# Far values: another order of seven block products, other buffers for two of x's sums, and near scores at later steps, in a hybrid attention and state-space layer

## Chip, cores and metric

The kernel runs on one core of a Trainium2 chip. The metric is the device time of one execution in microseconds (us); a kernel's time is the median of its runs. Engines are named as the profile names them: PE is TensorE (its weight loads are PEld), DVE is VectorE, ACT is ScalarE, POOL is GpSimd, SP is SyncE.

## What is computed

One decoder layer in float32 on 512 tokens of width 1024, cut here to what the change touches:

```python
proj = x @ w_in[layer]                       # q, k, v for 3 groups, ssm input, gate logits
q = apply_rope(q, pos); k = apply_rope(k, pos)
for g, (window, dilation) in enumerate(((128, 1), (512, 4), (2048, 16))):
    o_g, lse_g = dilated_group_attention(q[:, :, g], k[:, :, g], v[:, :, g], window, dilation)
attn = merge_by_softmax_denominators(outs, lses)
y_s = s5_ssm(u, ...)                         # complex diagonal scan, then GELU and GLU
mixed = gates[0] * (attn @ w_attn_br) + gates[1] * (y_s @ w_ssm_br)
h = layer_norm(ALPHA * x + mixed @ w_out)
out = layer_norm(ALPHA * h + swiglu(h))
```

Group 0 of the attention is called near, groups 1 and 2 are called far.

## The kernel before

**Precision and weights.** Each float32 operand of a matmul is split into a rounded part (hi) and a remainder (lo), and a product is three matmuls: hi by hi, hi by lo, lo by hi (line 207). A weight block of 128x1024 is prepared by a cast on ACT (names `whi…` and `wx…`) and a subtraction on DVE (`wlo…`, or the second half of `wx…`). SP loads the raw weights ahead. Prepared blocks lie in three pairs of buffers and, for the far values, in two borrowed ones, of which one is used once. When PE has used a block, `w.release()` gives its buffer to the next block in the list, so a block is prepared four units ahead of its use.

**Order of the work.** Every engine works through its own instructions in the order in which the code records them. The code goes through numbered steps: 4 to 28 are input projections, 28 to 36 the far values (7 products of 2 units each, 8/14 step a unit), 36 to 56 the other projections as five "quads" of 7 products (4/7 step a product), and after that come GLU, branch and output projections and the feed-forward part. `at_step(n, fn)` enters other work into this order: `fn` is recorded ahead of the first unit or product whose step is n or more.

**Far values.** The product of x with the value weights of groups 1 and 2 is made by blocks with seven products instead of eight (`v_product`, line 1205), numbered 1 to 7 and taken in the order of `VORDER` (line 1163). A product is 24 matmuls of 128x512, 12 for each unit. Products 1, 2 and 3 take blocks of x as they are. The others take sums of blocks: product 5 takes sum 0, product 7 sum 1, product 6 sum 2 and product 4 sum 3. A sum (`sum_x`, line 1081) is made by ACT, which negates a block (line 1085), and by an accumulating transfer from POOL's queue (line 1086). Sum 2 needs sum 0, and sum 3 needs sum 2. `split_x` (line 1088) then makes hi by a cast on ACT and lo by a subtraction on DVE. The results are `x_hi`, `x_lo` (sum 0, in the place of a block of x that is no longer needed), `x23h` and `x23l` (sums 1 and 2) and `x4` (sum 3, hi and lo in one buffer). The products add up in three pairs of PSUM banks, `vx`, `vy` and `vz`; `v_evict` (line 1217) copies or adds a bank into the values `v` after products.

The value weights are four raw blocks `rv0` to `rv3`, loaded at line 1169; `rv2` becomes `rv2 + rv3` by `sum_v` (line 1191) on DVE, and `prepare_v` (line 1174) makes the seven operands from these one by one, with three more sums in place. Products 1 and 6 use `rv0`, product 2 uses `rv1`, product 5 uses the summed `rv2`.

**The state output.** The state-space branch leaves its output `ysb` in the buffer `gat0`. Sixteen transfers on SP's queue write it to DRAM (`turn_y`, line 754, names `ydr<-ysb`), and it is fetched again much later. SP's next work behind them are the loads of the first quad's weights (line 1125, `rq`).

**Buffers.** Large buffers are named `big0` to `big8` and `gat0` to `gat3`; code asks for them by `home(n)`, and a table `swapped` renames some of them from step 24.9 on (`swap_homes`, line 246). Before, it exchanges 2 with 5, gat0 with 7 and 6 with 8. So `x23h` (home 5) lies in big2, `x23l` (home 7) in gat0, where `ysb` was, and `x4` (home 8) in big6, where one half of the states was. PE reads the states last in step 23.

**Near attention.** For each pair of heads j there are scores on PE (`attn_scores`, at `SCORES[0][j]`), then a masked maximum on DVE (line 848) and an exponential on ACT (line 850) for eight pieces, transposes on PE (`attn_turn`, at `WEIGHTS[0][j]`) and the product with the values at the step of the next scores. In the profile these are `s`, `un`, `t` and `o`.

Of the kernel before, what the change touches and what calls it, by code (L numbers as in the profile page):

```python
# [45 lines left out]
NSTR = 16  # L46


SCORES = [[33.8, 36.3, 39.1, 41.9, 44.7], [49.9, 52.5, 54, 55.7, 58.2]]
WEIGHTS = [[35.2, 38.1, 40.9, 43.7], [51, 53.2, 55, 57.2]]  # L50

# [120 lines left out]
def emit(ctx, tc, i, out):  # L174
# [65 lines left out]
    def home(n, name, dt=F32):  # L240
        n = swapped.get(n, n)
        return gat(n[1:], name, dt) if isinstance(n, str) else big(n, name, dt)

    swapped = {}

    def swap_homes():
        for a, b in ((2, 5), ("g0", 7), (6, 8)):
            swapped[a], swapped[b] = b, a

    w = Weights(nc, wp, split)  # L250
    out_homes = deque(("g0", 2, 6, 3))
# [727 lines left out]
    def at_step(n, fn, *a):  # L979
        fill.setdefault(n, []).append((fn, a))  # L980
# [41 lines left out]
    for kind in range(2):  # L1022
        for j, n in enumerate(SCORES[kind]):
            if j > 0:
                at_step(n, attn_values, kind, j - 1)
            if j < NPAIR:
                at_step(n, attn_scores, kind, j)
                at_step(WEIGHTS[kind][j], attn_turn, kind, j)
    xn = []
# [80 lines left out]
    at_step(24.4, sum_x, 0)  # L1110
    at_step(24.4, sum_x, 1)
    at_step(24.9, swap_homes)
    at_step(25.9, sum_x, 2)
    at_step(27.4, sum_x, 3)
    for n, at_ in enumerate((28.1, 27.2, 28.6, 29.6)):
        at_step(at_, split_x, n)


# [41 lines left out]

        w.after = rest

    VORDER = (1, 2, 5, 6, 3, 7, 4)
    vraw, vops, vslot, vbank = {}, {}, {}, {}
    vleft = deque((n, u) for n in VORDER for u in range(2))

# [166 lines left out]
    for g in (1, 2):  # L1333
        vs[g] = home((3, "g1", 0)[g], f"v{g}").rearrange("p (b c) -> p b c", b=4)
    for n, m in enumerate(VORDER):
        for u in range(2):
# [31 lines left out]
    for n in range(4):  # L1368
        ws = w.views[N_GLU + n]
        bs = []  # L1370
        for e in range(2):
            b = glu(f"gl{n}{e}")
# [323 lines left out]
    for e, m, nxt in (("b", 5, 6), ("a", 7, 4)):  # L1696
        at_ = dn_prep.index((m, 2))
# [321 lines left out]
def build(inputs):  # L2019
    import concourse.bacc as bacc  # L2020

    a = {k: np.asarray(v) for k, v in inputs.items()}
    arrays = {f"in_{k}": np.ascontiguousarray(v) for k, v in {**layout(a), **constants()}.items()}
    nc = bacc.Bacc("TRN2", target_bir_lowering=False, num_devices=1)
    aps = {k[3:]: nc.dram_tensor(k, v.shape, mybir.dt.from_np(v.dtype), kind="ExternalInput").ap()
           for k, v in arrays.items()}
    out = nc.dram_tensor("out_dram", (S, D), F32, kind="ExternalOutput").ap()
    with tile.TileContext(nc) as tc:
        with ExitStack() as ctx:
            with tc.manual_schedule():  # L2030
                emit(ctx, tc, aps, out)
    return nc, arrays
# [8 lines left out]
```

## Time and profile before

| what | us |
|---|---|
| median of three runs (827.59, 830.01, 830.37) | 830.01 |
| the profiled execution, its own time | 832.69 |
| its span, first to last instruction | 830.9 |
| PE busy within the span | 807.5 |
| DVE busy | 667.8 |
| ACT busy | 412.5 |

Between the span and the execution's own time lie 1.8 us. A row of a timeline gives start, duration, engine, line, operation, `out<-in` with the program's names (buffer numbers left out), shapes and a count; a bracket gives how long the engine had been idle and what ended that. Durations of neighbouring rows overlap a little, since instructions are pipelined; the distance between two starts is what an instruction adds to its engine's time. The chain's rows give start, duration, engine, name, line and count.

### The profile page before, as it was taken

What the parts mean: (1) busy time and instruction counts of PE and PEld (TensorE: products, weight loads), DVE (VectorE), ACT (ScalarE), POOL (GpSimd) and SP (SyncE); (2) the same over time, 40 slices, a digit from 0 to 9 for tenths busy, and PEclk for the clock granted to TensorE, in tenths of its full rate; (3) what the DMA queues carried; (4) which work ended last, traced back from release to release, by engine and by line L of the source; (5) the groups of instructions that cost most, each with busy time, mean ns of one, the idle gap of its engine ahead of it and who ended that gap; (6) DMA issues with size and microseconds to landing.
All of it is one profiled execution on the core that took longest, in us unless ns stands there. A gap on an engine that the chain in (4) does not pass through costs nothing.

```text
span 830.9 us, 13774 instructions
## 1 busy us (share of the span) xinstructions
PE 807.5 (97%) x5584; PEld 724.5 (87%) x5584; DVE 667.8 (80%) x1059; ACT 412.5 (50%) x607; POOL 80.2 (10%) x98
## 2 busy tenths in 40 slices
PE   9999999995999999999999999999999999999995
PEld 7888888874799999988888899999999999888884
DVE  6977997958768979746886699887777789789986
ACT  5973332543475645775334155554555445554520
POOL 0000002240003212300000230000000000020104
PEclk9999999996999999999999999999999999999998
DMA  8743438791225455762524225332223333774553
GB/s 335 188 112 123 144 121 250 184 202 25 101 96 104 105 133 128 173 234 95 209 103 166 86 78 177 114 141 102 103 103 106 109 116 114 276 173 147 148 130 102
DMA packets 32047, 117.48 MB, mean 141 GB/s; under 512 B 7664, under 2 KB 12528, under 8 KB 22512
## 3 DMA queue, kind: packets, MB, share of 16 engines
q1 hardware_dynamic: 23808, 91.83, 31.9%
q0 software_dynamic: 6544, 23.07, 13.4%
q10 hardware_dynamic: 1632, 1.70, 0.6%
q8 instruction: 44, 0.72, 0.3%
q14 instruction: 19, 0.16, 0.1%
HBM read 100.60 MB, written 9.70 MB: 133 GB/s over the span
## 4 chain that ended last, share of the span: by engine, by line
PE 89%; DVE 3%; DMA 3%; ACT 2%; SPq 1%; POOL 1%; issue 1%; DVEq 0%; ACTq 0%
PE qx L1258 7%; PE dnx L1798 5%; PE dnz L1798 4%; PE qz L1258 3%; PE pu L614 3%; PE pg L208 3%; PE pg L210 3%; PE pg L209 3%; PE dny L1798 2%; DMA ydr<-ysb 2%; PE wo L210 2%; PE wo L208 2%; PE b L208 2%; PE b L210 2%; PE b L209 2%; PE wo L209 2%
## 5 line engine op out<-in xcount | busy, mean ns | idle before, releaser
L1598 ACT CAST whi<-sums 128x1024 fp32r<-128x1024 f32 x40 | 41.9, 1048 | 66.2 <-DVE sums L349 66.2
L202 DVE TENSOR_TENSOR wlo<-raw,whi 128x1024 fp32r<-128x1024 f32 x44 | 54.2, 1235 | 17.7 <-ACT whi L201 17.7
L201 ACT CAST whi<-raw 128x1024 fp32r<-128x1024 f32 x44 | 45.9, 1048 | 22.9 <-PE pk L209 17.4
L349 DVE TENSOR_TENSOR wlo<-sums,whi 128x1024 fp32r<-128x1024 f32 x40 | 48.7, 1219 | 0.0
L349 DVE TENSOR_TENSOR wlo_q<-rq,whi_q 128x1024 fp32r<-128x1024 f32 x28 | 34.2, 1222 | 17.7 <-ACT whi_q L1153 17.6
L1153 ACT CAST whi_q<-rq 128x1024 fp32r<-128x1024 f32 x28 | 29.3, 1051 | 37.6 <-DVE rq L349 29.3
L1798 PE MATMUL dnx<-whi_d,pc 128*128 128x512 f32 (+1 forms) x128 | 38.2, 376 | 0.0
L775 POOL DMA_DIRECT2D kq<-qz x32 | 25.3, 1604 | 129.1 <-DVE qz L349 94.1
L208 PE MATMUL pg<-x_hi,whi 128*128 128x512 f32 x96 | 37.6, 392 | 0.0
L209 PE MATMUL pg<-x_lo,whi 128*128 128x512 f32 x96 | 37.4, 390 | 0.0
L210 PE MATMUL pg<-x_hi,wlo 128*128 128x512 f32 x96 | 37.4, 389 | 0.0
L850 ACT ACTIVATE un<-un,st 128x256 f32<-128x256 f32 (+1 forms) x64 | 30.8, 484 | 12.8 <-DVE st L848 12.8
L965 ACT ACTIVATE gt<-pg,bgate 128x512 f32<-128x512 f32 x12 | 8.3, 690 | 41.8 <-PE pg L210 41.8
L1710 ACT CAST whi_d<-dn 128x1024 fp32r<-128x1024 f32 x16 | 16.9, 1054 | 23.0 <-DVE dn L349 11.0
L1798 PEld LDWEIGHTS dnx<-whi_d,pc 128*128 128x128 f32 x128 | 23.6, 188 | 4.4
L1720 POOL DMA_DIRECT2D whi_db<-in_w_dp x3 | 1.7, 577 | 246.1 <-PE dny L1798 242.4
L349 DVE TENSOR_TENSOR wlo<-ra,whi 128x1024 fp32r<-128x1024 f32 x20 | 24.4, 1220 | 0.4 <-ACT whi L1598 0.4
L1798 PE MATMUL dnx<-wlo_d,pc 128*128 128x512 f32 (+1 forms) x64 | 24.1, 376 | 0.0
L1258 PE MATMUL qx<-x23h,whi_q 128*128 128x256 f32 x80 | 23.2, 290 | 0.0
L1258 PE MATMUL qz<-x_hi,whi_q 128*128 128x256 f32 x80 | 22.8, 286 | 0.0
L1258 PE MATMUL qz<-x_hi,wlo_q 128*128 128x256 f32 x80 | 22.6, 283 | 0.0
L1258 PE MATMUL qz<-x_lo,whi_q 128*128 128x256 f32 x80 | 22.6, 283 | 0.0
(838 smaller groups left out, 2985.4 us busy)
## 6 DMA issues: line engine op xcount, KB each, us to landing
raw<-in_w_in SPq DMA_DIRECT2D x12, 1024.0 KB, 5.3
ra<-in_w_gu SPq DMA_DIRECT2D x10, 1024.0 KB, 4.7
rb<-in_w_gu SPq DMA_DIRECT2D x10, 1024.0 KB, 4.8
rq<-in_w_quad SPq DMA_DIRECT2D x16, 512.0 KB, 4.0
dn<-in_w_dq SPq DMA_DIRECT2D x8, 1024.0 KB, 4.8
rv<-in_w_in SPq DMA_DIRECT2D x4, 1024.0 KB, 8.7
kq<-qz POOLq DMA_DIRECT2D x32, 128.0 KB, 5.0
raw<-in_w_br SPq DMA_DIRECT2D x4, 1024.0 KB, 4.9
```

What stands on the lines that cost most here:

```text
L201: act.copy(hi, src)
L202: dve.tensor_tensor(lo, src, hi.bitcast(F32), op=ALU.subtract)
L208: pe.matmul(dst, a[0], b[0], start=first, stop=False)
L209: pe.matmul(dst, a[0], b[1], start=False, stop=False)
L210: pe.matmul(dst, a[1], b[0], start=False, stop=last)
L349: eng.tensor_tensor(o, a, b, op=op)
L775: pool.dma_start(dst[32 * q : 32 * q + 32], z[32 * (q ^ 1) : 32 * (q ^ 1) + 32], accum_op=ALU.add)
L850: act.activation(pt, pt, AF.Exp, bias=mneg, scale=-1.0, accum_out=zsum)
L1153: act.copy(hi, src)
L1258: pe.matmul(d[:, 256 * e : 256 * e + 256], p_[:, e, k, :], q_[:, k, :], start=(first and e == k == m == 0), stop=(k == 3 and m == 2), skip ...
L1598: act.copy(hi, src)
L1798: pe.matmul(acc[key][0 if key == "v" else e][:, cs], p_, q_[:, cs], start=(key, e) not in begun, stop=(m == 2), skip_group_check=True)
```

## The change

Four tables or numbers change, and no operation is added or removed.

```diff
-SCORES = [[33.8, 36.3, 39.1, 41.9, 44.7], [49.9, 52.5, 54, 55.7, 58.2]]
-WEIGHTS = [[35.2, 38.1, 40.9, 43.7], [51, 53.2, 55, 57.2]]
+SCORES = [[34.8, 38.2, 40.5, 42.8, 45.1], [49.9, 52.5, 54, 55.7, 58.2]]
+WEIGHTS = [[37.1, 39.4, 41.7, 44], [51, 53.2, 55, 57.2]]
...
     def swap_homes():
-        for a, b in ((2, 5), ("g0", 7), (6, 8)):
-            swapped[a], swapped[b] = b, a
+        swapped.update({2: 5, 5: 2, "g0": 7, 7: 6, 6: 8, 8: "g0"})
...
-    at_step(25.9, sum_x, 2)
-    at_step(27.4, sum_x, 3)
-    for n, at_ in enumerate((28.1, 27.2, 28.6, 29.6)):
+    at_step(26.4, sum_x, 2)
+    at_step(28.9, sum_x, 3)
+    for n, at_ in enumerate((28, 28.5, 30.2, 32)):
         at_step(at_, split_x, n)
...
-    VORDER = (1, 2, 5, 6, 3, 7, 4)
+    VORDER = (1, 5, 2, 6, 3, 7, 4)
```

Products 2 and 5 change places. `x23l` now lies in big6 and `x4` in gat0; `x23h` stays in big2. The negations for sums 2 and 3 and the four splits are recorded at other steps. The first near scores stand ahead of product 4 instead of between the two units of product 7; each of the four transposes stands two quad products behind its scores (the first: two units and two products), where three products (the first: two units) lay between them before.

On DVE, at the place where the far values begin, the rows before were these (`v20` is product 2, unit 0, and so on; `kq`, `zq` are the rotary products of the last two projections, `pq10` and `pq11`).

```order
L349 TENSOR_TENSOR wlo0_v20_1718<-rv1_1658,whi0_v20_1717 128x1024
L349 TENSOR_TENSOR kq01_1484<-pq11_1756,rope_130 128x4x128
L349 TENSOR_TENSOR zq10_1749<-pq11_1756,rope_130 128x4x128
L349 TENSOR_TENSOR wlo1_v21_1753<-rv1_1658,whi1_v21_1752 128x1024
L349 TENSOR_TENSOR rv0_1491<-rv2_1332,rv0_1491 128x1024
L349 TENSOR_TENSOR wlo2_v50_1788<-rv2_1332,whi2_v50_1787 128x1024
L349 TENSOR_TENSOR x23l_1793<-xf1_1582,x23h_1792 128x1024
L349 TENSOR_TENSOR rv0_1491<-rv2_1332,rv0_1491 128x1024
L349 TENSOR_TENSOR wx_v51_1816<-rv2_1332,wx_v51_1816 128x1024
L349 TENSOR_TENSOR x_lo0_95<-xf0_1580,x_hi0_93 128x4x256
```

After, in the same place (the changed file is one line shorter, so line 349 is 348 there), with the rows from the last subtraction of product 1 on:

```order
L348 TENSOR_TENSOR wx_v11_1666<-rv0_1491,wx_v11_1666 128x1024
L348 TENSOR_TENSOR rv0_1491<-rv2_1332,rv0_1491 128x1024
L348 TENSOR_TENSOR rv2_1332<-rv2_1332,rv3_1526 128x1024
L348 TENSOR_TENSOR kq01_1484<-pq10_1722,rope_130 128x4x128
L348 TENSOR_TENSOR zq10_1748<-pq10_1722,rope_130 128x4x128
L348 TENSOR_TENSOR wlo0_v50_1718<-rv2_1332,whi0_v50_1717 128x1024
L348 TENSOR_TENSOR rv0_1491<-rv2_1332,rv0_1491 128x1024
L348 TENSOR_TENSOR kq01_1484<-pq11_1758,rope_130 128x4x128
L348 TENSOR_TENSOR zq10_1748<-pq11_1758,rope_130 128x4x128
L348 TENSOR_TENSOR wlo1_v51_1752<-rv2_1332,whi1_v51_1751 128x1024
L348 TENSOR_TENSOR wlo2_v20_1790<-rv1_1658,whi2_v20_1789 128x1024
L348 TENSOR_TENSOR x_lo0_95<-xf0_1580,x_hi0_93 128x4x256
```

`x_lo0` now stands ahead of `x23l`, and the two sums of `rv0` have moved ahead of it as well.

On ACT, the rows of the same place before (`xf0`, `xf1` are the buffers in which the sums are made):

```order
L1100 CAST whi0_v20_1717<-rv1_1658 128x1024
L1085 ACTIVATE xf1_1582<-xf0_1580 128x1024
L1100 CAST whi1_v21_1752<-rv1_1658 128x1024
L1100 CAST whi2_v50_1787<-rv2_1332 128x1024
L1100 CAST x23h_1792<-xf1_1582 128x1024
L1085 ACTIVATE xf0_1580<-xf1_1582 128x1024
L1100 CAST wx_v51_1816<-rv2_1332 128x1024
L1100 CAST x_hi0_93<-xf0_1580 128x4x256
```

After, from the first cast of product 5 to the cast of product 6's first unit:

```order
L1099 CAST whi0_v50_1717<-rv2_1332 128x1024
L1099 CAST whi1_v51_1751<-rv2_1332 128x1024
L1084 ACTIVATE xf1_1582<-xf0_1580 128x1024
L1099 CAST whi2_v20_1789<-rv1_1658 128x1024
L1099 CAST x_hi0_93<-xf0_1580 128x4x256
L1099 CAST wx_v21_1811<-rv1_1658 128x1024
L1099 CAST x23h_1815<-xf1_1582 128x1024
L1221 COPY v1_1794<-vx0_1797 128x512
L1221 COPY v1_1794<-vx7_1798 128x512
L1084 ACTIVATE xf0_1580<-xf1_1582 128x1024
L1099 CAST whi0_v60_1850<-rv0_1491 128x1024
```

The casts from `rv2` stand ahead of those from `rv1`, and `x_hi0` stands ahead of `x23h`.

Further on in ACT's order after, the cast of sum 3 into gat0 stands between a cast for product 7 and the copies behind product 6:

```order
L1099 CAST wx_v31_1908<-rv1_1658 128x1024
L1099 CAST whi0_v70_1928<-rv2_1332 128x1024
L1099 CAST x4_1817<-xf0_1580 128x1024
L1227 COPY v1_1794<-vx0_1797 128x512
L1227 COPY v1_1794<-vx7_1798 128x512
L1099 CAST whi1_v71_1948<-rv2_1332 128x1024
```

Before, it stood directly behind the first cast for product 6, ahead of the second. It is now the first instruction that writes into the buffer of the state output.

## The prediction

> **What bounds the kernel now.** I read the page first, then PE's waits, then the timelines of PE, DVE, ACT and SP around the longest of them. The page says that PE is busy nearly all the time:
>
> ```profile
> span 830.9 us, 13774 instructions
> PE 807.5 (97%) x5584; PEld 724.5 (87%) x5584; DVE 667.8 (80%) x1059; ACT 412.5 (50%) x607; POOL 80.2 (10%) x98
> ```
>
> So time can only come from PE's waits or from matmuls that run slowly. PE's waits (engine, what waited, for whom: us in total, times, longest) are few:
>
> ```profile
> PE vz L1214 <- DVE x_lo L349: 9.3, 1, 9.3
> PE vz L1214 <- ACT x_hi L1100: 1.3, 1, 1.3
> ...
> PE vx L1214 <- ACT un L850: 0.9, 1, 0.9
> ```
>
> All three stand among the far values. PE's timeline there:
>
> ```profile
> 178.83 0.39 PE L1214 MATMUL vy<-whi_v,x_hi 128*128 128x512 f32 x1
> ...
> 184.04 0.39 PE L1214 MATMUL vy<-whi_v,x_lo 128*128 128x512 f32 x1
> 185.77 0.50 PE L1214 MATMUL vz<-whi_v,x_hi 128*128 128x512 f32 x1 [1.34 <-ACT x_hi L1100]
> 186.11 0.40 PE L1214 MATMUL vz<-wlo_v,x_hi 128*128 128x512 f32 x1
> 195.76 0.80 PE L1214 MATMUL vz<-whi_v,x_lo 128*128 128x512 f32 x1 [9.26 <-DVE x_lo L349]
> ...
> 203.67 0.39 PE L1214 MATMUL vx<-whi_v,x23h 128*128 128x512 f32 x1
> ```
>
> The first and last of the 24 matmuls of product 2 start 5.21 us apart: 0.2265 us a matmul, 5.44 us a product. Product 5 should therefore have run from 184.27 to 189.71; product 6 started at 203.67. **Product 5 lost 13.96 us**: 11.0 until its third matmul (195.76 instead of 184.72), and 2.92 because the 22 matmuls from there took 7.91 us instead of 4.99. The window with the slow ones (PE busy, then the granted clock, DMA share, GB/s) shows why:
>
> ```profile
> 196.00:202.00 6.00, 6.00 (x15) 0.53 0.00 0
> ```
>
> The clock was 0.53 after the long wait. The chain from PE goes to `x_lo` on DVE, and DVE was held:
>
> ```profile
> 167.03 1.22 DVE L349 TENSOR_TENSOR wx_v<-rv,wx_v 128x1024 fp32r<-128x1024 f32 x1
> 168.16 1.22 DVE L349 TENSOR_TENSOR rv<-rv,rv 128x1024 f32<-128x1024 f32 x1
> 169.29 1.07 DVE L349 TENSOR_TENSOR kq<-pq,rope 128x512 f32<-128x512 f32 x1
> 170.18 1.08 DVE L349 TENSOR_TENSOR zq<-pq,rope 128x512 f32<-128x512 f32 x1
> ...
> 175.51 1.09 DVE L349 TENSOR_TENSOR kq<-pq,rope 128x512 f32<-128x512 f32 x1
> 176.43 1.10 DVE L349 TENSOR_TENSOR zq<-pq,rope 128x512 f32<-128x512 f32 x1
> 177.37 1.22 DVE L349 TENSOR_TENSOR wlo_v<-rv,whi_v 128x1024 fp32r<-128x1024 f32 x1
> ...
> 191.08 1.23 DVE L349 TENSOR_TENSOR x23l<-xf,x23h 128x1024 fp32r<-128x1024 f32 x1 [10.23 <-DMA ydr<-ysb]
> ...
> 194.49 1.22 DVE L349 TENSOR_TENSOR x_lo<-xf,x_hi 128x1024 fp32r<-128x1024 f32 x1
> ```
>
> `x23l` is written over `ysb`, so it waited 10.23 us for the transfers of the state output; `x_lo` stood three instructions behind it. SP's row shows how long the sixteen transfers were being issued, and ACT's rows show the two waits that made `x_hi` late:
>
> ```profile
> 163.28 22.18 SPq L761 DMA_DIRECT2D ydr<-ysb  x16
> ```
>
> ```profile
> 173.28 1.05 ACT L1100 CAST whi_v<-rv 128x1024 fp32r<-128x1024 f32 x1 [9.42 <-DMA rv<-in_w_in]
> 174.24 1.05 ACT L1085 ACTIVATE xf<-xf 128x1024 f32<-128x1024 f32 x1
> ...
> 181.83 1.05 ACT L1100 CAST x23h<-xf 128x1024 fp32r<-128x1024 f32 x1 [4.65 <-DMA xf<-in_xk]
> ...
> 184.68 1.04 ACT L1100 CAST x_hi<-xf 128x1024 fp32r<-128x1024 f32 x1
> ```
>
> ACT stood 9.42 us for `rv1`, although `rv2` was there, and then 4.65 us for sum 2, with `x_hi` queued behind.
>
> **The change part by part.** *Buffers.* `x23l` goes to big6, whose last reader (the states) was done in step 23: its wait is gone. The state output's buffer is now first written by ACT's cast `x4`. ACT comes to it behind `whi0_v70`, whose buffer product 6's first unit frees. By the times below that unit ends at 193.0, so the cast is reached at 194.1, and the transfers had landed by 191.08. So this wait costs nothing, with 3 us to spare. The waiting cast would hold the copies behind product 6 and `whi1_v71`, which PE wants only at 203.9 (product 6 starts at 190.3, product 7 two products of 5.44 later at 201.2, and its second unit 2.72 after that).
>
> *`x_lo`.* Its new place on DVE comes by adding distances of starts: 1.13 for a 128x1024 subtraction or sum (167.03 to 168.16), 0.89 to 0.94 for `kq` and `zq` (169.29 to 170.18, 175.51 to 176.43 to 177.37). From `wx_v11` at 167.03: `rv0` 168.16, `rv2` 169.29, `kq` 170.42, `zq` 171.31, `wlo0_v50` 172.25, `rv0` 173.38, `kq` 174.51 (its projection ends at 173.4), `zq` 175.43, `wlo1_v51` 176.37, `wlo2_v20` 177.50, `x_lo` 178.63, done at 179.85. What ACT owes it is ready: `whi2_v20` follows `rv1` at about 173.4, `x_hi` at 174.4. PE starts product 5 at 178.83 and wants `x_lo` for its third matmul at 179.28. **A wait of 0.57 us remains.** It may be nothing if DVE gains half a microsecond, or 1.7 if one more pass of 1.13 gets in front. Whether so short a wait brings the clock down is answered by the third wait of PE (the DVE row is the add that PE stood for):
>
> ```profile
> 221.72 0.39 PE L1214 MATMUL vx<-whi_v,x23l 128*128 128x512 f32 x1
> 223.00 0.47 PE L1214 MATMUL vx<-whi_v,x 128*128 128x512 f32 x1 [0.89 <-ACT un L850]
> 223.31 0.40 PE L1214 MATMUL vx<-wlo_v,x 128*128 128x512 f32 x1
> 223.54 0.62 PE L1214 MATMUL vx<-whi_v,x 128*128 128x512 f32 x2
> ```
>
> ```profile
> 222.17 1.28 DVE L349 TENSOR_TENSOR v<-v,vx 128x512 f32<-128x512 f32 x2
> ```
>
> After 0.89 us idle the matmuls start 0.31 and 0.23 apart, so the clock held. I take 0.57 and no more.
>
> [...]
>
> *The wait in row 223.00.* Product 4 starts 1.05 us after the last matmul of product 7 should have ended (221.95). It adds to the bank that DVE must first add to the values, behind the softmax of scores recorded in between. After, DVE's two adds come before that softmax, and PE does the scores meanwhile (1.72 us as below, against 1.28 for the adds of both banks). So 1.05 goes; if that cover failed, it would stay.
>
> *Sum 2 and sum 3.* Sum 2's negation stands behind `whi1_v51`, whose raw sum ends at 170.5; that cast and the negation end at 172.5, against 175.3 before (row 174.24). POOL's queue keeps its order. Its transfers took this long from issue to landing:
>
> ```profile
> L1086 POOL DMA_DIRECT2D xf<-in_xk x4: 880/927/932, 161.3 to 184.1; - x4
> ...
> DMA to landing us min/median/max: 5.3/6.3/10.3
> ```
>
> Issued at 172.8, sum 2 lands at 178 to 183. Behind it on ACT come `x23h`, two copies, the negation for sum 3 and `whi0_v60`, then `wlo0_v60` on DVE: 5.6 us at the rows' durations, so 184 to 189. PE wants it at 178.83 + 0.57 + 10.88 = 190.3. Nothing waits even at 10.3, up to a landing of 12. Sum 3 is issued behind `x23h`, some 10 us after sum 2, and is wanted behind product 7, at 206.6, by product 4.
>
> *Loads and near scores.* The loads of `rq` wait for DVE's last use of `rv0` and `rv1`, now at 193 to 197; nothing else is in SP's queue then, and the first quad's operand has no free buffer before 203.9. Scores and transposes cost PE what they cost before. But the softmax between them gets two quad products instead of three:
>
> ```profile
> 234.82 1.72 PE s L837 x16
> 236.54 3.07 PE qz L1258 x24
> 239.61 2.88 PE qx L1258 x24
> ```
>
> ```profile
> 241.88 0.49 ACT L850 ACTIVATE un<-un,st 128x256 f32<-128x256 f32 x1
> ```
>
> The last exponential ended at 242.37, 5.83 us after the scores; two products are 5.95. The first transposes need only the first pieces. I put this at 0, with 0 to 1 us at each of three places as its bounds.
>
> **Sum.** 13.96 + 1.05 - 0.57 = 14.4 us. The profiled execution took 832.69 us (1.8 more than its span) and would take 818.3. It lies 2.7 above the median of the runs, and nothing ties that to this stretch; so I take 14.4 off the median: 830.01 - 14.4 = **815.6 us**.
>
> **Rivals.** *B, `x_lo` is later still.* One more pass or a late `rv1` makes the wait 1.7 us, and the clock falls as it did after the long one: 1.1 + 2.92 = 4.0 lost, 819.6 us. For it: DVE has no gap from 167 on. Against: the 0.89 us wait that left the clock alone. [...]
>
> *C, sum 2 is late.* It is now issued among the state output's and the rotary transfers; one of the four such transfers took 10.3 us before. Twice that, 20.6, would be 8.6 us past the slack of 12; with 2.92 of clock that is 11.5 lost, 827.1 us. Against: no such landing in the trace.
>
> *D, slower: the near softmax becomes PE's wait.* Its place is the last three near transposes. If the lag of 5.83 grew to about 9 us at each, PE would wait 3.1 and then lose 2.92 of clock, three times 6.0, or 18.1 in all: 833.7 us. It decides against the change from a lag of 7.8 on, where 1.9 + 2.92 at three places eats the 14.4. Against it: DVE and ACT have the same work to do between scores and transposes as before, apart from its order. [...]
>
> *E, the change only moves the wait.* If the state output's transfers landed after some 203 instead of 191, ACT's `x4` would hold the casts for products 7 and 4, and each further microsecond would be PE's; at 218 all is given back: about 830. Against: the transfers are issued at the same place in SP's queue as before.
>
> **Chances.** Forecast 0.79, B 0.10, C 0.05, D 0.03, E 0.03. A measurement of this kernel can tell about 0.3%, 2.5 us, from no change. Forecast, B and most of C are faster, E and a rest of C the same, D slower: 0.93, 0.04, 0.03. The range begins 3 us under the forecast (no wait for `x_lo`, and the 2.4 us by which the lowest run of before lay under its median) and reaches through B to 821.
>
> **What would show it.** Right: no wait of `x23l` for `ydr`; `x_lo` on DVE before 181; PE's waits among the far values under 1 us; no slice with a lower clock in the middle; the first quad product 14 to 15 us earlier. Wrong: a PE wait of over 2 us for `x_lo`, `x23h` or `un`, a clock under 0.9 between 170 and 300 us, or ACT standing before `x4`.

## The result, and the profile after

| kernel | runs | median, us | lowest to highest, us |
|---|---|---|---|
| before | 4 | 830.19 | 827.59 to 830.74 |
| after | 4 | 818.35 | 818.27 to 818.59 |

After to before is 0.9864 (95% interval 0.9843 to 0.9885): 11.8 us faster by the medians. The two profiled executions differ by more, 832.69 against 818.33 us, or 14.36 us.

The page of the kernel after: the span is 14.4 us shorter, and PE is busy 3.7 us less although it does the same 5584 matmuls; most of that is the 2.92 us of slow matmuls.

```profile
span 816.5 us, 13783 instructions
PE 803.8 (98%) x5584; PEld 721.8 (88%) x5584; DVE 667.2 (82%) x1059; ACT 411.9 (50%) x607; POOL 80.3 (10%) x98
```

PE's longest waits after, but for one at the kernel's very start, which was there before (engine, what waited, for whom: total us, times, longest). The wait for `x_lo` is down from 9.3 to 0.5, and those for `x_hi` and at product 4 (`un`) are gone. No wait among the near scores has come up, so rival D has no place:

```profile
...
PE vz L1213 <- DVE x_lo L348: 0.5, 1, 0.5
PE yc L732 <- DVE ysb L348: 0.5, 1, 0.5
PE qx L1257 <- DVE qssw L348: 0.4, 1, 0.4
```

PE's timeline after, from the start of product 5 to that of product 6, with product 2 between them now:

```profile
178.53 0.39 PE L1213 MATMUL vz<-whi_v,x_hi 128*128 128x512 f32 x1
178.76 0.39 PE L1213 MATMUL vz<-wlo_v,x_hi 128*128 128x512 f32 x1
179.67 0.50 PE L1213 MATMUL vz<-whi_v,x_lo 128*128 128x512 f32 x1 [0.52 <-DVE x_lo L348]
180.01 0.40 PE L1213 MATMUL vz<-whi_v,x_hi 128*128 128x512 f32 x1
...
190.23 0.39 PE L1213 MATMUL vx<-whi_v,x23h 128*128 128x512 f32 x1
```

Two products take 10.88 us at the 0.2265 us a matmul of product 2 in before, and here, at a granted clock of 1.00 from 176 to 212, they took 190.23 - 178.53 = 11.70. So **0.82 us is still lost**: 0.69 until the third matmul (179.67 instead of 178.98), and the rest behind it, where the next start comes 0.34 us later instead of 0.23.

DVE after. `x_lo` runs at 178.41, where the prediction put it at 178.63. `x23l` no longer stands ahead of it, and waits for nothing but its own hi part:

```profile
178.41 1.21 DVE L348 TENSOR_TENSOR x_lo<-xf,x_hi 128x1024 fp32r<-128x1024 f32 x1
...
185.13 1.23 DVE L348 TENSOR_TENSOR x23l<-xf,x23h 128x1024 fp32r<-128x1024 f32 x1 [4.38 <-ACT x23h L1099]
...
188.00 1.23 DVE L348 TENSOR_TENSOR wlo_v<-rv,whi_v 128x1024 fp32r<-128x1024 f32 x1 [0.51 <-ACT whi_v L1099]
```

The last row is the first lo of product 6. It ends at 189.23, and PE wants it one matmul after 190.23: 1.2 us to spare. ACT after, and POOL's issue of sum 2:

```profile
174.07 1.05 ACT L1099 CAST x_hi<-xf 128x1024 fp32r<-128x1024 f32 x1
...
184.05 1.05 ACT L1099 CAST x23h<-xf 128x1024 fp32r<-128x1024 f32 x1 [6.92 <-DMA xf<-in_xk]
...
194.83 1.04 ACT L1099 CAST x<-xf 128x1024 fp32r<-128x1024 f32 x1
```

```profile
172.68 0.93 POOL L1085 DMA_DIRECT2D xf<-in_xk  x1 [1.98 <-ACT xf L1084]
```

The wait for sum 2 has moved from before `x_hi` to behind it, where PE has other work. The cast of sum 3 into the state output's old buffer (194.83) stands behind no wait. The near scores fill the gap ahead of product 4 (last matmul of product 7, scores, product 4):

```profile
206.71 0.39 PE L1213 MATMUL vx<-whi_v,x23l 128*128 128x512 f32 x1
207.03 1.79 PE L836 MATMUL s<-kq 64*128 64x128 f32 x16
208.74 0.50 PE L1213 MATMUL vx<-whi_v,x 128*128 128x512 f32 x1
```

So the sum in the profiled executions is 13.96 - 0.82 + 1.05 = 14.2, plus 0.30 because the first of these products starts at 178.53 instead of 178.83: 14.5, where 14.36 were gained.

### The profile page after: what moved, and what is told of

It reads as the page before. It is cut to its first block, busy times and chain, and to the rows that moved or that the text cites. A ratio compares the mean times of both kernels' runs of the same rounds, so it can differ in the third digit from the quotient of the medians.

```text
span 816.5 us, 13783 instructions
## 1 busy us (share of the span) xinstructions
PE 803.8 (98%) x5584; PEld 721.8 (88%) x5584; DVE 667.2 (82%) x1059; ACT 411.9 (50%) x607; POOL 80.3 (10%) x98
## 4 chain that ended last, share of the span: by engine, by line
PE 89%; DVE 5%; ACT 2%; issue 1%; POOL 1%; DMA 1%; DVEq 0%; SPq 0%; ACTq 0%
PE qx L1257 7%; PE dnx L1797 5%; PE dnz L1797 4%; PE qz L1257 3%; PE pg L208 3%; PE pg L209 3%; PE pg L210 3%; PE pu L613 2%; PE dny L1797 2%; PE wo L210 2%; PE wo L209 2%; PE b L210 2%; PE b L209 2%; PE wo L208 2%; PE b L208 2%; PE s L836 2%
## 5 line engine op out<-in xcount | busy, mean ns | idle before, releaser
L1257 PE MATMUL qx<-x23h,wlo_q 128*128 128x256 f32 x80 | 22.6, 283 | 0.0
```

The costliest lines, as they stand in the source:

```text
L1257: pe.matmul(d[:, 256 * e : 256 * e + 256], p_[:, e, k, :], q_[:, k, :], start=(first and e == k == m == 0), stop=(k == 3 and m == 2), skip ...
```

## The experiments

**The theory.** PE lost 14 us because `x_lo` stood behind `x23l`, which waited for the state output's transfers, and because the clock fell behind that wait. The new order takes `x_lo` out of that queue and `x_hi` out of the queue for sum 2; the new buffer takes `x23l` out of its wait. **The rivals.** Either half alone does all of it; or the time comes from the near scores; and for the 2.6 us between 14.4 and 11.8, that the stall in before is not always as long as in its first profile. "After" is here 818.35 and 818.33 us (median and profiled execution).

### The buffers alone

The kernel before, with:

```diff
 def swap_homes():
-    for a, b in ((2, 5), ("g0", 7), (6, 8)):
-        swapped[a], swapped[b] = b, a
+    swapped.update({2: 5, 5: 2, "g0": 7, 7: 6, 6: 8, 8: "g0"})
```

> The kernel before with the new places of the two sums alone; order of the products, steps and scores stay. Theory (the wait for the state output's transfers is the loss, and the order only what is left): x23l starts behind x23h at about 183, the sum of rv0 and the subtraction of wx_v51 follow, and x_lo, now behind the cast x_hi (row 184.68), runs from 185.9 to 187.1. PE still waits 1.3 us for x_hi, then 0.5 to 1 us for x_lo instead of 9.3, and the clock stays at 1.00. Product 5 loses 2.3 us instead of 13.96, and the 1.05 at product 4 stays: 11.6 us less than the profiled execution of before, 821 us, 2.8 over the kernel after. Rival (the order does it, the buffer is incidental): x_hi and x_lo stay late, PE waits over 5 us, and the time stays within 3 us of before. Rival (x4 only takes over the wait): ACT stands before x4 past 192 and PE waits for the second unit of product 6.

Measured 825.28 us (six runs, 823.35 to 826.14) beside 832.11 for before: 0.9922 (0.9904 to 0.994). The theory's 821 was missed by 4 us. PE's timeline of this kernel:

```profile
187.50 0.79 PE L1213 MATMUL vz<-whi_v,x_hi 128*128 128x512 f32 x1 [3.50 <-ACT x_hi L1099]
188.09 0.63 PE L1213 MATMUL vz<-wlo_v,x_hi 128*128 128x512 f32 x1
189.32 0.79 PE L1213 MATMUL vz<-whi_v,x_lo 128*128 128x512 f32 x1 [0.61 <-DVE x_lo L348]
...
196.49 0.39 PE L1213 MATMUL vx<-whi_v,x23h 128*128 128x512 f32 x1
```

ACT's rows give the reason:

```profile
183.56 1.05 ACT L1099 CAST x23h<-xf 128x1024 fp32r<-128x1024 f32 x1 [7.29 <-DMA xf<-in_xk]
...
186.40 1.04 ACT L1099 CAST x_hi<-xf 128x1024 fp32r<-128x1024 f32 x1
```

The wait for `x_lo` is 0.61, as expected. But `x_hi` still stands behind `x23h`, and sum 2's reader started at 183.56, not at 181.83 as in the first profile. So PE waited 3.50 us for `x_hi`, and the next matmul starts 0.59 us behind it: the clock had fallen, to 0.50 in the windows from 188 to 192. So the buffer alone is not enough.

### The old buffers in the new order

The kernel after, with:

```diff
 def swap_homes():
-    swapped.update({2: 5, 5: 2, "g0": 7, 7: 6, 6: 8, 8: "g0"})
+    for a, b in ((2, 5), ("g0", 7), (6, 8)):
+        swapped[a], swapped[b] = b, a
```

> The kernel after with the old places of the two sums; order, steps and scores as after. Theory: x_lo stays on time (PE waits 0.5 us for it), but x23l stands behind the state output's transfers until about 191, and the first lo of product 6, 2.9 us behind it on DVE, is done at about 195.2, where PE wants it at 190.5: a wait of 4.7 us, and up to 2.9 us more if the clock falls. 823 to 826 us. Rival (the new order alone does it): 818 to 819, no wait over 1 us.

Measured 820.95 us (820.35 to 821.95, before 832.11): 0.9875 (0.9857 to 0.9892). PE's and DVE's rows:

```profile
191.19 0.50 PE L1214 MATMUL vx<-wlo_v,x23h 128*128 128x512 f32 x1 [0.55 <-DVE wlo_v L349]
...
198.07 0.50 PE L1214 MATMUL vz<-wlo_v,x_hi 128*128 128x512 f32 x1 [1.14 <-DVE wlo_v L349]
```

```profile
187.64 1.23 DVE L349 TENSOR_TENSOR x23l<-xf,x23h 128x1024 fp32r<-128x1024 f32 x1 [6.89 <-ACT v L1226]
```

The mechanism is there, and its size was wrong: `x23l` got its buffer at 187.64, not at 191. It delays DVE's subtractions for two products, and PE waits 0.55 and 1.14. (The bracket names ACT's copy of `v`, the last event that the profile has ahead of the start. `x23l` doesn't read it, and its hi part was done at 183.5. What else it waits for are the state output's transfers: the last of the sixteen was issued at 185.1, and none of this output's transfers took under 2.2 us to land, so it was there at 187.3 at the earliest, 0.3 us ahead of the start.) So the order alone, with the scores, gave 11.2 of the gain in this comparison. To the 818.35 of the first comparison it is another 2.6, which is then the buffers'; the profiled executions, 820.98 and 818.33, say the same.

### The scores alone, and without them

The kernel before, with:

```diff
-SCORES = [[33.8, 36.3, 39.1, 41.9, 44.7], [49.9, 52.5, 54, 55.7, 58.2]]
-WEIGHTS = [[35.2, 38.1, 40.9, 43.7], [51, 53.2, 55, 57.2]]
+SCORES = [[34.8, 38.2, 40.5, 42.8, 45.1], [49.9, 52.5, 54, 55.7, 58.2]]
+WEIGHTS = [[37.1, 39.4, 41.7, 44], [51, 53.2, 55, 57.2]]
```

> The kernel before with the new steps of the near scores and transposes alone. Theory: only the wait of 0.89 us at the start of product 4 goes, so 1.05 us less than before, 829 us, with the stall at product 5 unchanged (within what before's runs scatter). If two quad products do not cover the softmax, up to 1 us at each of three places comes back: no gain or up to 2 us slower.

Measured 829.46 us (twelve runs, 826.88 to 832.19; before 832.11): 0.9973 (0.9958 to 0.9989), so 0.9 to 3.5 us faster. That holds the 1.05, but the medians can't confirm it, since both kernels scatter by 5 us; its profiled execution is taken up at the end of this part. The other way round, the kernel after with the old two lines:

> The kernel after with the old steps of the near scores and transposes. Theory: PE's wait at the start of product 4 is back, behind the add that stands behind the first softmax: 1.05 us over after, 819.4 us, and nothing else changes. If the later transposes cost PE waits that the profile of after does not show as such, it would be faster than after instead.

Measured 819.4 us (five runs, 819.01 to 820.89): 1.05 over the 818.35 of the kernel after, which ran in another comparison; the profiled executions, 819.40 and 818.33, differ by 1.07. PE's waits have the one at product 4 again:

```profile
PE vx L1213 <- ACT un L849: 0.9, 1, 0.9
```

Wait, profiled execution and median agree on the term. The wait is the strongest of the three, since the runs overlap with later ones of after (817.98 to 820.30, below).

### How long a wait costs clock

The subtraction for `x_lo` is repeated in the kernel after (twice, three times, five times in all).

```diff
         src = (h1[:, 0:4], h2[:, 4:8], h2[:, 0:4], h1[:, 4:8])[n]
         two_steps(src, hi, lo)
+        if n == 0:
+            w.after = lambda: [tt(lo, src, hi.bitcast(F32), ALU.subtract) for _ in range(3)]
```

The new line stands behind `two_steps`, whose own single subtraction it replaces.

> The kernel after with the subtraction that makes x_lo done three times, to the same result: nothing is left out, DVE has two more passes of 1.13 us at that place. It asks from what length on a wait of PE costs clock. PE's wait for x_lo should grow from 0.5 to about 2.8 us. If a wait of that length leaves the clock alone: 2.3 us over after, 820.6 us, granted clock 1.00 behind it. If it falls as behind the 9.3 us wait of before (2.92 us lost in slow matmuls): 823.5 us. [...]

> The kernel after with the subtraction that makes x_lo done five times, to the same result: four more passes of 1.13 us on DVE, nothing left out. PE's wait for x_lo should be about 5.0 us. If the clock falls as behind the 9.3 us wait of before: 4.5 + 2.9, 825.7 us, with a stretch at about half clock. If it holds: 822.8 us. [...]

> The kernel after with the subtraction that makes x_lo done twice, to the same result; nothing is left out. PE's wait for x_lo should be about 1.7 us, the wait of the prediction's rival B. If a wait of that length leaves the clock alone: 1.1 us over after, 819.5 us. If the clock falls for one stretch of 3.4 us, as in the run with three times: 1.7 us more, 821.2. If as behind the long wait of before: 2.9 more, 822.4. Were the length of the wait all that decides, all runs would agree; if the place of the wait in a window that runs on its own decides, as the slow stretches of 3.4, 6.8, 6.8, 6.8, 10.2 and 13.6 us in the runs so far suggest, runs may differ by 1.7.

| subtraction | wait in the profile, us | profiled execution, us | all runs, us |
|---|---|---|---|
| once (after) | 0.52 | 818.33 | 818.27 to 818.59 |
| twice | 1.79 | 821.38 | 821.38, 821.15; 819.93, 819.81, 819.55, 819.16 |
| three times | 3.08 | 821.91 | 822.93, 822.06, 822.04, 821.91; 820.41 |
| five times | 5.57 | 825.70 | 824.66 to 825.71 |

Three times was to take 820.6 or 823.5 us, and its median, 822.04, lies between; five times was to take 825.7 with a falling clock, and its median is 825.50. With two passes the runs fall into two groups, 1.2 to 2.2 us apart. The profiled execution is of the upper one. Its PE timeline, and then its windows (PE, PEld, DVE, ACT and POOL busy, granted clock, DMA share, GB/s):

```profile
180.93 0.50 PE L1215 MATMUL vz<-whi_v,x_lo 128*128 128x512 f32 x1 [1.79 <-DVE x_lo L348]
181.27 0.40 PE L1215 MATMUL vz<-whi_v,x_hi 128*128 128x512 f32 x1
181.51 0.46 PE L1215 MATMUL vz<-wlo_v,x_hi 128*128 128x512 f32 x1
181.76 0.63 PE L1215 MATMUL vz<-whi_v,x_lo 128*128 128x512 f32 x1
```

```profile
180.00:182.00 2.00, 1.07 (x4) 0.91 (x5) 2.00 (x2) 0.00 (x0) 0.05 (x1) 0.93 0.99 164
182.00:184.00 2.00, 2.00 (x6) 1.54 (x6) 0.13 (x2) 1.20 (x2) 0.00 (x0) 0.50 1.02 157
184.00:186.00 2.00, 2.00 (x8) 1.61 (x7) 2.00 (x2) 2.00 (x4) 0.00 (x0) 0.72 0.64 124
```

The windows in the middle of a slow stretch read 0.50 and those outside it 1.00, so I read a value between as a mean of the two, and it tells when the clock changed. In the first row (1 - 0.93) / 0.5 of 2 us, or 0.28, was slow: it fell at 181.72, after the wait had ended. In the last (1 - 0.72) / 0.5 of 2 us, or 1.12: it came back at 185.12, after **3.40 us**. The same from the windows of the other kernels:

| profiled execution | clock fell, us | came back, us | slow for, us |
|---|---|---|---|
| before, first profile | 188.04 | 201.68 | 13.64 |
| before, second | 189.08 | 199.32 | 10.24 |
| before, third | 188.28 | 201.96 | 13.68 |
| scores alone | 189.32 | 196.12 | 6.80 |
| buffers alone | 186.88 | 193.68 | 6.80 |
| `x_lo` twice | 181.72 | 185.12 | 3.40 |
| three times | 182.60 | 186.04 | 3.44 |
| five times | 182.80 | 189.60 | 6.80 |

For instance the three-times kernel:

```profile
182.00:184.00 2.00, 2.00 (x7) 1.54 (x8) 1.53 (x2) 1.66 (x3) 0.00 (x0) 0.65 0.76 129
184.00:186.00 2.00, 2.00 (x6) 1.61 (x5) 1.78 (x2) 1.38 (x3) 0.39 (x1) 0.50 0.40 84
186.00:188.00 2.00, 2.00 (x10) 1.58 (x10) 0.99 (x1) 1.53 (x2) 0.54 (x1) 0.99 0.70 110
```

Every slow stretch is one, two, three or four times 3.41 us, within 0.04, which is what 0.01 of clock in a row makes. The 3.41 is the mean: the eight add up to 64.80 us, nineteen times that. At the end of the kernel, where PE's last matmul starts at 820.67, the clock falls once more. In the first profile of before that is

```profile
822.00:824.00 2.00, 0.00 (x0) 0.00 (x0) 1.92 (x5) 0.00 (x0) 0.99 (x1) 0.73 0.82 192
```

or at 822.92, which is 634.88 us after the fall at 188.04, or 186.2 times 3.41. What sets these lengths and the moment of a fall was not shown.

The shortest wait behind which a window shows a fall is the 1.79 us of the two-times kernel. The longest that stood alone among the far values and behind which the windows stay at 1.00 is 1.14 us, in the kernel with the old buffers (1.00 from 196 to 202).

The cost, estimated from these readings, is half of what PE works within the slow stretch. In before PE worked from 195.76 to 201.68 at half clock, 5.92 us, and lost 2.96 by that, against the 2.92 read from the distance of the matmuls. In the two-times kernel PE worked through all of the 3.40 us, its starts 0.43 apart instead of 0.23 (181.76 to 182.19), which makes 1.70; its profiled execution took 3.05 more than that of after (821.38 and 818.33) for 1.27 us more of waiting, which leaves 1.78. That its lower group kept its clock is argued from the times, which are 0.8 to 1.6 over after for 1.27 us more of waiting; none of them was profiled, and whether the place of the wait decided it was not shown. The same holds for the 820.41 of the three-times kernel, 2.1 over after for 2.56 us more of waiting.

### The sums of `rv0` behind `x_lo`

The kernel after, with:

```diff
-        if n == 5:
-            tt(a11, a21, a11, ALU.subtract)
+        if (n, u) == (2, 1):
+            for c in (slice(0, 1024), slice(1024, 2048)):
+                tt(vraw[0][:, c], vraw[2][:, c], vraw[0][:, c], ALU.subtract)
```

> The kernel after with the two sums of rv0, which stand ahead of x_lo on DVE and are wanted only by product 6, behind x_lo instead. Theory: x_lo is done 2.26 us earlier, unless x_hi on ACT (done at 175.1) holds it, and the last wait of 0.5 us at product 5 goes; product 6's first lo has 1.2 us of slack and DVE stands idle 4.4 us before x23l, so nothing is late behind it: 0.5 us under after, 817.8 us. Rival (the wait moves to product 6): its lo is late by up to a microsecond, 818.3 to 819.

> The kernel after with the two sums of rv0 behind x_lo on DVE, once more, beside the kernel after on the same chip. Theory: the wait of 0.5 us at product 5 is gone and nothing takes its place: 0.4 to 0.6 us under the kernel after. Rival: product 5 starts later by as much as the wait was long, or another wait grows: no difference of over 0.2 us.

> The kernel after unchanged, beside before on the same chip and for another profile. Theory: no instruction before product 4 waits for a transfer's landing any more, so its runs agree within half a microsecond, at 818.3, and before's scatter over 5 us comes from the stall alone. Rival: after scatters too where sum 2 lands later than 184.

| kernel | comparison | median, us | lowest to highest, us | after to before, or this to before |
|---|---|---|---|---|
| `rv0` later | first | 817.94 | 817.36 to 820.27 | 0.9839 (0.9811 to 0.9867) |
| `rv0` later | second | 817.77 | 817.35 to 819.49 | 0.9843 (0.9817 to 0.987) |
| after | second | 818.19 | 817.98 to 820.30 | 0.9851 (0.9825 to 0.9878) |

DVE and PE of the second:

```profile
177.66 1.21 DVE L348 TENSOR_TENSOR x_lo<-xf,x_hi 128x1024 fp32r<-128x1024 f32 x1
```

```profile
178.75 0.39 PE L1214 MATMUL vz<-whi_v,x_hi 128*128 128x512 f32 x1
178.98 0.39 PE L1214 MATMUL vz<-wlo_v,x_hi 128*128 128x512 f32 x1
179.21 0.39 PE L1214 MATMUL vz<-whi_v,x_lo 128*128 128x512 f32 x1
...
189.63 0.39 PE L1214 MATMUL vx<-whi_v,x23h 128*128 128x512 f32 x1
```

`x_lo` is done at 178.87, and the third matmul wants it at 179.21: the last wait is gone, and two products take 10.88 us, without loss. It starts 0.75 us earlier than in after, not 2.26, for the most part because DVE now stands for a rotary product's projection ahead of it, 1.18 us in the profile of the first. The median is 0.4 us lower beside after on the same chip. That is in the size expected, but the ranges overlap, so the trace shows it better than the time does. By its medians it is the fastest version here.

The theory for after's runs was only half right: three of five lie at 818.0 to 818.2, the others at 819.35 and 820.30. Their listed clocks, 0.997 and 0.996, are no lower than the others'. What they wait for was not profiled and stays open; sum 2, with 1.2 us to spare behind it, is the first place to look.

### Before, twice more

> The kernel before unchanged, for another profile. Its runs lie between 827.6 and 832.7 us, those of after within 0.3. Theory: the length of the stall differs, because x23l waits for transfers whose landing and PE's clock behind the wait vary; then in an execution of 830 us product 5 loses some 11 us instead of 13.96, and everything else has the same length. Rival: the stall is 13.96 us again whatever the time, and the difference lies elsewhere in the program, so that the 14.4 taken off the median was mis-sized for another reason.

> The kernel before unchanged, for a third profile. Theory: its time differs from the other two profiled executions (832.69 and 830.26 us) by what product 5 lost (13.96 and 11.96 us): the start of x23l, when the last of the state output's transfers has landed, sets when x_lo is done and PE goes on, and the slow stretch behind is a whole number of 3.4 us. Rival: time and stall do not go together.

DVE and PE of the second profile of before, an execution of 830.26 us:

```profile
188.60 1.23 DVE L349 TENSOR_TENSOR x23l<-xf,x23h 128x1024 fp32r<-128x1024 f32 x1 [7.24 <-ACT whi_v L1100]
...
192.01 1.22 DVE L349 TENSOR_TENSOR x_lo<-xf,x_hi 128x1024 fp32r<-128x1024 f32 x1
```

```profile
183.62 0.39 PE L1214 MATMUL vy<-whi_v,x_lo 128*128 128x512 f32 x1
185.66 0.50 PE L1214 MATMUL vz<-whi_v,x_hi 128*128 128x512 f32 x1 [1.66 <-ACT x_hi L1100]
...
193.29 0.80 PE L1214 MATMUL vz<-whi_v,x_lo 128*128 128x512 f32 x1 [6.89 <-DVE x_lo L349]
...
201.24 0.39 PE L1214 MATMUL vx<-whi_v,x23h 128*128 128x512 f32 x1
```

The first of these PE rows is the last matmul of product 2. Product 5 should have run for 5.44 us from 183.85 on, and product 6 should have started at 189.29; it lost 201.24 - 189.29 = 11.95 us. In the third profile, of 833.38 us:

```profile
192.09 1.22 DVE L349 TENSOR_TENSOR x23l<-xf,x23h 128x1024 fp32r<-128x1024 f32 x1 [10.43 <-DMA ydr<-ysb]
```

There product 5 lost 14.74 in the same reckoning (183.91 to 204.32).

| before | `x23l` starts, us | product 5 lost, us | execution, us | execution less the loss |
|---|---|---|---|---|
| second profile | 188.60 | 11.95 | 830.26 | 818.31 |
| first profile | 191.08 | 13.96 | 832.69 | 818.73 |
| third profile | 192.09 | 14.74 | 833.38 | 818.64 |

Time and stall go together: the executions lie 3.1 us apart, and without the stall 0.4. What varies is when the state output's transfers have landed. The last of the sixteen was issued at 181.7, 184.6 and 184.0 us (second, first and third profile), and `x23l` starts 6.9, 6.5 and 8.1 us behind that. In the first profile this transfer took 6.1 us to land, which is 190.7, and `x23l` starts 0.3 us later; in the other two the transfers of this output, its later fetch among them, took 2.7 to 13.0 and 2.9 to 13.2 us. (In the second profile the bracket of `x23l` names ACT's cast `whi_v`, which it doesn't read.)

The same reckoning holds for the profiled executions of the kernels that change a part of before. With the buffers alone product 5 lost 7.21 us (183.61 to 196.49), and 825.37 less that is 818.16, 0.15 under the lowest of the table. With the scores alone it lost 10.18 (183.65 to 199.50), and 827.18 less that is 817.00: 1.3 to 1.7 below the three of before, where the wait at product 4 should be worth 1.05.

The 43 runs of before in four comparisons reach from 827.59 to 834.15, with a median of 831.45; the nine of after from 817.98 to 820.30, with a median of 818.33. By these medians the gain is 13.1 us.

## Why the prediction was right, and where it was off

**The stall at product 5** (13.96, of which 0.57 was to stay): right, with 0.82 staying, 0.25 more than forecast: the third matmul started 0.69 late, and the fourth 0.34 behind it instead of 0.23. Its place, its cause and the two mechanisms (the DVE queue behind `x23l`, the ACT queue behind `x23h`) are what the runs with one half each show: with the buffers alone PE still waits 3.50 for `x_hi`, with the order alone 0.55 and 1.14 for the subtractions of products 6 and 3.

**The 1.05 at product 4**: right; with the old tables in the kernel after, the wait of 0.9 and 1.05 us came back.

**The 0 for the near softmax and for `x4`**: right; neither stands in any wait of after. Sum 2 took from its issue at 172.68 until just before 184.05, some 11.4 us, more than the 10.3 that the prediction had as the longest, and still within its slack of 12.

**What was off is the base of the subtraction**: "It lies 2.7 above the median of the runs, and nothing ties that to this stretch; so I take 14.4 off the median". The second and third profile of before tie it to this stretch. The long execution had the long stall, so the 14.4 belonged to 832.69 alone, and that gives 818.3, where after lies. The one profiled at 830 had a stall of some 12. Taken off the median the sum was too large by 2.7 us, which is within what the stall varies. Two kinds of luck are in this. That 832.69 less 14.4 meets the profiled 818.33 so closely is in part luck: 0.25 us more than forecast was lost at product 5, and 0.30 was gained ahead of it, for which the sum had no term. And that the measured 818.35 still lies in the range is owed to its upper end, which was set at 821 for rival B, and B did not happen.

**The rivals.** B's wait of 1.7 us was made on purpose, and was 1.79 in the profile: there the clock fell for 3.40 us, which cost 1.7, not 2.92, and by their times it held in four of the six runs. The argument against B, the 0.89 us wait that left the clock alone (1.00 from 212 to 230), holds for waits of that length alone: it says nothing of 1.7. The 2.92 belongs to the stretch of 13.64 us in before, of which PE worked through the last 5.92 alone. C, D and E did not happen.

## What to carry to other kernels

A term that depends on when a transfer lands belongs to the execution in which it was read: subtract it from that execution's time, or profile the kernel again before taking it off a median; the scatter of the kernel before (6.6 us in 43 runs) was itself a sign that its longest wait was for something irregular (`x23l` started at 188.60, 191.08 and 192.09). When an operand waits in an engine's queue behind work for later products, try the order of the queue and the buffer apart: here the order, with the scores, took away most of the loss (11.2 us) and the other buffer what then came next (2.6), and each alone left a wait of its own (1.14 and 3.50). To measure a small term, undo it in the steadier version, not in the one that scatters more.

## What was not expected of the hardware

The clock's slow stretches in eight profiled executions, 3.40 to 13.68 us long, lay within 0.04 of whole multiples of 3.41 us, and one of 3.40 followed a wait of 1.79 us, while behind waits of 0.52 (after), 0.89 (before) and 0.55 and 1.14 us (the kernel with the old buffers) among the far values the windows stayed at 1.00. The landing of the same sixteen transfers varied: in the three profiles of before the instruction that waited for them started at 188.60, 191.08 and 192.09. Sum 2 behaved alike: in the three profiles of before it was issued at 175.59 to 176.40 and its reader started at 181.72 to 182.41; in after it was issued at 172.68 and 172.46 and its reader started at 184.05 and 183.89, and in the other kernels with the new order it was issued at 171.8 to 172.7 and its reader started at 182.3 to 183.9. Issued 2.9 to 3.9 us earlier in after than in before, among the state output's transfers, it landed no earlier. Why the transfers take such different times was not tried and stays open.
